# One core: the high part of V's differences moves from ScalarE to GpSimd, and scores are emitted in parts

## Chip, core and metric

The kernel runs on one core of a Trainium2 chip. The time is device microseconds of one execution; the table further down has the median of three runs and the one execution that the profiler recorded. The core's engines work side by side, each through its own queue in order: TensorE (PE in the views; PEld are its weight loads), VectorE (DVE), ScalarE (ACT), GpSimd (POOL) and SyncE (SP), which here issues the DMAs.

## What is computed

A two-layer decoder trunk on 1024 tokens of width 1024: a Mamba-2 layer, then stick-breaking attention with 16 heads of 64, and after each layer a gated per-layer embedding. The change lies in the attention:

```python
z = jnp.einsum('bhtd,bhsd->bhts', q[:, :, q0:kend], k[:, :, :kend])
strict = s_idx < t_idx
log_keep = jnp.where(strict, jax.nn.log_sigmoid(-z), 0.0)
suffix = lax.cumsum(log_keep, axis=3, reverse=True) - log_keep
weights = jnp.where(strict, jnp.exp(jax.nn.log_sigmoid(z) + suffix), 0.0)
outs.append(jnp.einsum('bhts,bhsd->bhtd', weights, v[:, :, :kend]))
```

A weight is the difference of two neighbouring running products of sigmoid(-z). The kernel therefore never forms the weights: it makes the running products (a scan over the keys) and multiplies them with differences of neighbouring rows of V.

## The kernel before

Every matrix product that must be accurate is made of three TensorE products of a high and a low part: a number is rounded to a shorter form (the high part, `...h`), and the rest is the low part (`...l`).

Attention runs over 8 head pairs `hp`, and within a pair over 4 steps p = 3, 2, 1, 0 of 256 tokens each: 32 steps. Tokens are stored in reverse, so the scores of block b run over (8 - b) x 128 keys: 128 and 256 keys at p=3, 384 and 512 at p=2, 640 and 768 at p=1, 896 and 1024 at p=0, for each of the two heads. The steps are pipelined in code order, in `step(i)`:

- *Fill*: for step i, `project` (k, q and v of two token blocks, 24 matmuls each in four groups of six; ScalarE copies k and q out as `kq`, VectorE v as `vr`), and for p=3 and p=2 `gate` (24 matmuls). After these come `values` and `norm`.
- `values` makes V's differences: three DMAs on SP's queue shift `vr` by one row into `vs`, GpSimd subtracts (L853), ScalarE copies the high parts of `V` (L858, two copies of 128x128), GpSimd makes the low parts (L859). `product` reads this V for the first time two steps later.
- `norm` normalizes k and q on VectorE, by a dozen small instructions (`kss`, `krv`, `kry`, `krs`) and a product into `kq` (L870).
- *Pieces*, put between the groups of the fill by their place between 0 and 1: for step i-1 `flip` (four transposes of `kq`, L879, then ScalarE and VectorE write `kst`, `qh`, `ql`) at `FLIP`, and four `scores` spread over `SPREAD[1]`; for step i-2 the turns and products, spread over `SPREAD[0]`. What has a place beyond the last group comes after `values` and `norm`.
- `scores` (L893 to L905): for each half of a wide row, two matmuls into a PSUM tile `z` (two buffers), a sigmoid on ScalarE into `pt` (L903); then one scan over the row on VectorE (L904).
- `turn` (L907): three or four transposes of `pt` on TensorE into a PSUM tile `tr` (L916, L919; two buffers, shared with `flip`), a copy `wh` on ScalarE (L925), a low part `wl` on VectorE (L926). `product` (L936) multiplies both with V; `fold` (L947 to L953) combines the heads into `GT`.

The weights of the next pair are loaded during p=2 and p=1 and split into `g0h` (ScalarE, L104) and `g0l` (VectorE, L108). The order on each engine is the order that a scheduler makes of this code; each engine then runs its own list in order.

Of the kernel before, what the change touches and what calls it, by code (L numbers as in the profile page):

```python
# [8 lines left out]
F32 = mybir.dt.float32  # L9
# [4 lines left out]
ALU = mybir.AluOpType  # L14
# [4 lines left out]
P = 128  # L19
S = 1024  # L20
# [13 lines left out]
NEX = 5  # L34
EARLY = 3
LASTP = ((0, 0, 512), (1, 0, 256), (1, 256, 256))
SPREAD = ((0.05, 0.95), (0.7, 1.0))
FLIP = 0.55
FILL = {32: (7, (4, 5, 6, 7)), 33: (6, ())}
CHUNKS = {30: (0, 1, 2, 3)}  # L40

# [742 lines left out]
def attention(k, A, rawp, hT, oTd, dbg, b2, pairs):  # L784


    tc, nc = k.tc, k.nc
# [3 lines left out]
    with ExitStack() as ctx:  # L791
        pp = ctx.enter_context(tc.tile_pool(name="b_pair", bufs=1, reuse_waits="tile"))
        wk = ctx.enter_context(tc.tile_pool(name="b_work", bufs=2, reuse_waits="tile"))
# [6 lines left out]
        keep = pp.tile([P, S], BF16, name="keep")  # L800
# [7 lines left out]
        def begin_pair(st):  # L808
            st["V"], st["vr"], st["v0"] = {}, {}, {}
            st["GT"] = pairs.gt.tile([P, S], F32, name="GT")  # L810

        def project(st, b):
            W = st["W"]
            ps = mm.tile([P, 512], F32, name="mm")
            prs = []
            sl = slice(b % 4 * P, b % 4 * P + P)
            for kk in range(KT):
                whi, wlo = W[kk]
                prs += terms((hh[b // 4][:, kk, sl], hl[b // 4][:, kk, sl]), (whi[:, :384], wlo[:, :384]))
            yield from split3_some(nc, ps[:, :384], prs, 6)  # L820
            p = b // 2
            if b % 2:
                st["kq"] = wk.tile([P, 2, 2, P], F32, name="kq", bufs=2)
                st["vr"][p] = wk.tile([P, 2, P], F32, name="vr", bufs=3)
            nc.scalar.copy(st["kq"][:, b % 2], ps.rearrange("p (m c) -> p m c", c=256)[:, :, 0:128])
            nc.vector.tensor_copy(st["vr"][p][:, b % 2], ps[:, 128:256])
            yield

        def gate(st, half):
            W = st["W"]  # L830
            gp = mm.tile([P, 512], F32, name="mm")
            sl = slice(half * 512, half * 512 + 512)
            prs = []
            for kk in range(KT):
                whi, wlo = W[kk]
                prs += terms((whi[:, 384:], wlo[:, 384:]), (hh[half][:, kk], hl[half][:, kk]))
            yield from split3_some(nc, gp, prs, 4)
            sg = wk.tile([P, 512], F32, name="sg", bufs=1)
            nc.scalar.activation(sg, gp, AF.Sigmoid)
            nc.vector.tensor_tensor(st["GT"][:, sl], gp, sg, op=ALU.mult)  # L840
            yield

        def values(st, p):

            vr = st["vr"][p]
            vs = wk.tile([P, 2, P], F32, name="vs", bufs=1)
            nc.sync.dma_start(vs[0:P - 1], vr[1:P])
            nc.sync.dma_start(vs[P - 1:P, 0], vr[0:1, 1])
            nc.sync.dma_start(vs[P - 1:P, 1], st["vr"][p + 1][0:1, 0] if p < 3 else zrow)
            st["v0"][p] = sm.tile([P, 2], F32, name="v0", bufs=4)  # L850
            for i in range(2):
                nc.sync.dma_start(st["v0"][p][:, i:i + 1], vr[0:1, i])
            nc.gpsimd.tensor_tensor(vs, vs, vr, op=ALU.subtract)  # L853
            V = st["V"][p] = wk.tile([P, 2, 256], F32R, name="V", bufs=6)
            Vx = V.rearrange("p b (x c) -> p b x c", c=64)
            d = vs.rearrange("p b (h c) -> p b h c", c=64)
            for i in range(2):
                nc.scalar.copy(Vx[:, i, 0::3], d[:, i])  # L858
                nc.gpsimd.tensor_tensor(Vx[:, i, 1:3], d[:, i], Vx[:, i, 0::3].bitcast(F32), op=ALU.subtract)  # L859

        def norm(st, p):
# [11 lines left out]
        def flip(st, p):  # L873
            kn = st.pop(("kn", p))
            tsl = slice(p * 256, (p + 1) * 256)
            tq = trp.tile([P, 512], F32, name="tr")
            for i in range(2):
                for m in range(2):
                    nc.tensor.transpose(tq[:, m * 256 + i * P:m * 256 + (i + 1) * P], kn[:, i, m], ident)  # L879
            kt, qt = tq[:, 0:256], tq[:, 256:512]  # L880
            qh = wk.tile([P, 2, 256], F32R, name="qh", bufs=1)
            for h in range(2):
                o, x = own[h], own[1 - h]
                g = k.gkq[o]
                nc.scalar.activation(kst[o, h, tsl], kt[o], AF.Copy, scale=g)
                nc.vector.scalar_tensor_tensor(
                    kst[x, h, tsl], kt[o], g, kst[o, h, tsl].bitcast(F32), op0=ALU.mult, op1=ALU.subtract)
                nc.scalar.copy(qh[o, h], qt[o])
                nc.scalar.copy(qh[x, h], qt[o])
                nc.vector.tensor_tensor(ql[o, h], qt[o], qh[o, h].bitcast(F32), op=ALU.subtract)  # L890
            st["q", p] = qh

        def scores(st, h, b):  # L893
            qh = st["q", b // 2]
            N = (NT - b) * P
            qs = slice((b % 2) * P, (b % 2) * P + P)
            pt = wk.tile([P, S], F32, name="pt", bufs=5)
            for ko, n in ([(0, N)] if N <= 512 else [(0, N // 2), (N // 2, N // 2)]):
                z = zp.tile([P, 512], F32, name="z")
                rk = kst[:, h, b * P + ko:b * P + ko + n]  # L900
                nc.tensor.matmul(z[:, :n], lhsT=qh[:, h, qs], rhs=rk, start=True, stop=False)
                nc.tensor.matmul(z[:, :n], lhsT=ql[:, h, qs], rhs=rk, start=False, stop=True)
                nc.scalar.activation(pt[:, ko:ko + n], z[:, :n], AF.Sigmoid, scale=-1.0)  # L903
            nc.vector.tensor_tensor_scan(pt[:, :N], pt[:, :N], keep[:, :N], 1.0, op0=ALU.mult, op1=ALU.max)  # L904
            st["a", h, b] = pt  # L905

        def turn(st, p, h, j0):  # L907

# [57 lines left out]
        n = len(steps)  # L966

        def spread(fns, a, z):
            m = len(fns)
            return [(a + (z - a) * (i + 0.5) / m, f) for i, f in enumerate(fns)]  # L970

        def combine_pieces(st, p):

            units = [(h, j) for h in range(2) for j in range(2 * p, NT, 2)]
            def prod(h, j):
                product(st, p, h, j)
                if j == NT - 2:
                    fold(st, p, h)
            fns = []
            for i, (h, j) in enumerate(units):  # L980
                fns.append(lambda h=h, j=j: turn(st, p, h, j))
                if i >= 2:
                    fns.append(lambda u=units[i - 2]: prod(*u))
            return fns + [lambda u=u: prod(*u) for u in units[-2:]]

        def step(i):
            pieces = []
            if i >= 2:
                hp, p = steps[i - 2]
                pieces += spread(combine_pieces(sts[hp], p), *SPREAD[0])  # L990
            if 1 <= i <= n:
                hp, p = steps[i - 1]
                st = sts[hp]
                pieces.append((FLIP, lambda st=st, p=p: flip(st, p)))
                units = [(lambda st=st, h=h, b=b: scores(st, h, b)) for h in range(2) for b in (2 * p + 1, 2 * p)]
                pieces += spread(units, *SPREAD[1])
            pieces.sort(key=lambda x: x[0])
            fill = []
            if i < n:
                hp, p = steps[i]  # L1000
                if p == NT // 2 - 1:
                    pairs.all(hp)
                    begin_pair(sts[hp])
                    if hp + 1 < 8:
                        pairs.start(hp + 1)
                    else:
                        b2.begin(pairs)
                fill = [(project(sts[hp], 2 * p + 1), 5)]
                if p >= 2:
                    fill.append((gate(sts[hp], p - 2), 7))  # L1010
                fill.append((project(sts[hp], 2 * p), 5))
            total = sum(w for _, w in fill)
            done = 0
            for f, w in fill:
                for _ in f:
                    done += 1
                    while pieces and pieces[0][0] <= done / total:
                        pieces.pop(0)[1]()
            if i < n:
                if p in LOADS:  # L1020
                    pairs.step(hp + 1)
                values(sts[hp], p)
                norm(sts[hp], p)
                if i in CHUNKS:
                    b2.weights(CHUNKS[i])
            for _, f in pieces:
                f()
# [226 lines left out]
```

## Time and profile before

| what | value |
|---|---|
| median of 3 runs | 1968.46 us (1967.15 to 1968.69) |
| profiled execution | 1969.7 us |
| its span, first to last instruction | 1968.0 us |
| TensorE busy | 1773.3 us, 90% |
| VectorE busy | 1173.5 us, 60% |
| ScalarE busy | 902.1 us, 46% |
| GpSimd busy | 378.1 us, 19% |
| mean granted TensorE clock | 0.952 |

The span holds the Mamba layer, the embedding, then the attention from some 940 to 1740 us, and the last embedding. Busy shares are means over stages that differ; for the change the attention stage counts alone. A busy TensorE isn't TensorE at its peak: the granted clock says which part of its full speed it had (1.00 is 2.4 GHz, 0.50 is 1.2 GHz). Where a row ends in brackets, the first number in them is the idle time of the engine before that instruction, and behind `<-` stands what ended it.

### The profile page before, as it was taken

To read this page: it belongs to the slowest core of one execution; us is meant where nothing else is said; L and a number is where in the kernel's file an instruction comes from. 1 tells how busy PE (TensorE), PEld (TensorE's weight loads), DVE (VectorE), ACT (ScalarE), POOL (GpSimd) and SP (SyncE) were. 2 spreads that over 40 slices of the span, in tenths; PEclk is the share of its full clock that TensorE was granted. 3 is DMA by queue.
4 is the path that set the end of the run, shared out by engine and by line. 5 is a ranking of instruction groups with operands and counts; after the bars stand their busy time and mean duration, and the time that the engine had idled before them with its cause. 6 is when DMAs were issued, how large, how long until landed. Compare 5 with 4: busy or idle time off the path is not lost.

```text
span 1968.0 us, 25316 instructions
## 1 busy us (share of the span) xinstructions
PE 1773.3 (90%) x9170; PEld 1496.2 (76%) x9170; DVE 1173.5 (60%) x2462; ACT 902.1 (46%) x1974; POOL 378.1 (19%) x384
## 2 busy tenths in 40 slices
PE   7999999999999999999888888888888887679999
PEld 6778878878867778888877777777777776557887
DVE  6685484493596543456476757676767666664332
ACT  5566375375473321244363535353545443542121
POOL 0245445345342222000000000000000001111110
PEclk9999999999999999999989888989898988889999
DMA  4222222232126543222010101010101011223110
GB/s 145 72 84 94 70 86 82 69 93 91 59 92 207 165 144 118 88 86 97 9 57 18 48 17 48 18 47 18 48 18 48 18 37 53 66 86 98 58 49 32
DMA packets 96396, 139.41 MB, mean 71 GB/s; under 512 B 18160, under 2 KB 66640, under 8 KB 96272
## 3 DMA queue, kind: packets, MB, share of 16 engines
q1 hardware_dynamic: 96272, 137.80, 21.8%
q8 instruction: 72, 1.18, 0.2%
q14 instruction: 52, 0.43, 0.1%
HBM read 108.77 MB, written 24.77 MB: 68 GB/s over the span
## 4 chain that ended last, share of the span: by engine, by line
PE 61%; DMA 15%; DVE 13%; ACT 7%; issue 2%; POOL 2%; POOLq 0%; SPq 0%; DVEq 0%; ACTq 0%
PE mm L46 38%; DMA vs<-vr 13%; PE mm L53 9%; DVE pt L904 3%; PE pq L46 2%; PE oq L936 2%; DVE v L234 2%; PE intra L409 2%; PE tr L916 1%; DVE wl L926 1%; POOL vs L853 1%; PE inter L404 1%; PE tr L664 1%; ACT pt L903 1%; PE tr L919 1%
## 5 line engine op out<-in xcount | busy, mean ns | idle before, releaser
L46 PE MATMUL mm<-ul,wh 128*128 128x512 f32 (+1 forms) x648 | 254.0, 392 | 0.0
L46 PE MATMUL mm<-uh,wl 128*128 128x512 f32 (+1 forms) x648 | 252.5, 390 | 0.0
L46 PE MATMUL mm<-uh,wh 128*128 128x512 f32 (+1 forms) x648 | 252.4, 389 | 0.1
L904 DVE TENSOR_TENSOR_SCAN pt<-pt,keep 128x128 f32<-128x128 f32 (+7 forms) x128 | 175.4, 1374 | 55.3 <-ACT pt L903 54.9
L53 PE MATMUL mm<-g0h,hh 128*128 128x384 f32 x512 | 191.4, 374 | 3.6 <-ACT g0h L104 2.9
L53 PE MATMUL mm<-g0l,hh 128*128 128x384 f32 x512 | 179.4, 350 | 1.9 <-DVE g0l L108 1.9
L53 PE MATMUL mm<-g0h,hl 128*128 128x384 f32 x512 | 179.0, 350 | 0.0
L916 PE MATMUL tr<-ident,pt 128*128 128x128 f32 x320 | 82.6, 306 | 104.7 <-DVE wl L926 102.2
L926 DVE TENSOR_TENSOR wl<-tr,wh 128x512 fp32r<-128x512 f32 (+1 forms) x160 | 101.3, 634 | 121.5 <-ACT wh L925 119.1
L234 DVE SCALAR_TENSOR_TENSOR v<-u,convh,v 128x512 f32<-128x512 f32 x144 | 130.1, 909 | 55.1 <-ACT v L232 52.6
L853 POOL TENSOR_TENSOR vs<-vs,vr 128x256 f32<-128x256 f32 x32 | 23.3, 728 | 682.7 <-DMA vs<-vr 654.8
L925 ACT CAST wh<-tr 128x512 fp32r<-128x512 f32 (+1 forms) x160 | 85.0, 543 | 126.2 <-PE tr L919 124.6
L46 PEld LDWEIGHTS mm<-ul,wh 128*128 128x128 f32 x648 | 121.7, 188 | 26.4 <-issue 2.3
L46 PEld LDWEIGHTS mm<-uh,wl 128*128 128x128 f32 x648 | 121.8, 188 | 25.7 <-issue 1.9
L46 PEld LDWEIGHTS mm<-uh,wh 128*128 128x128 f32 x648 | 121.7, 188 | 25.4 <-issue 1.1
L916 PEld LDWEIGHTS tr<-ident,pt 128*128 128x128 f32 x320 | 48.1, 154 | 118.9 <-DVE wl L926 110.4
L106 POOL TENSOR_TENSOR wl<-raw,wh 128x1024 fp32r<-128x1024 f32 x39 | 95.3, 2443 | 155.6 <-ACT wh L104 148.9
L53 PEld LDWEIGHTS mm<-g0h,hh 128*128 128x128 f32 x512 | 101.3, 198 | 4.5 <-ACT g0h L104 3.2
L53 PEld LDWEIGHTS mm<-g0l,hh 128*128 128x128 f32 x512 | 101.9, 199 | 2.8 <-DVE g0l L108 2.1
L858 ACT CAST V<-vs 128x128 fp32r<-128x128 f32 x64 | 15.9, 295 | 191.7 <-POOL vs L853 191.7
L53 PEld LDWEIGHTS mm<-g0h,hl 128*128 128x128 f32 x512 | 101.6, 198 | 0.6
L574 DVE SCALAR_TENSOR_TENSOR acc<-mm,rg,acc 128x512 f32<-128x512 f32 x64 | 47.7, 748 | 84.1 <-PE mm L46 83.3
(350 smaller groups left out, 4427.6 us busy)
## 6 DMA issues: line engine op xcount, KB each, us to landing
raw<-in_w_in SPq DMA_DIRECT2D x40, 512.0 KB
ex<-acd SPq DMA_DIRECT2D x64, 256.0 KB
raw<-in_w_b SPq DMA_DIRECT2D x32, 512.0 KB
raw<-in_m_out SPq DMA_DIRECT2D x16, 512.0 KB
raw<-in_gate SPq DMA_DIRECT2D x16, 512.0 KB
graw<-gT SPq DMA_DIRECT2D x30, 256.0 KB
gT<-zs SPq DMA_DIRECT2D x28, 256.0 KB
acc<-in_x SPq DMA_DIRECT2D x8, 512.0 KB
```

The source lines that it names most:

```text
L46: nc.tensor.matmul(out, lhsT=a, rhs=b, start=(i == 0), stop=(i == n - 1))
L53: nc.tensor.matmul(out, lhsT=a, rhs=b, start=(i == 0), stop=(i == n - 1))
L106: (eng or nc.gpsimd).tensor_tensor(lo, raw, hi.bitcast(F32), op=ALU.subtract)
L234: nc.vector.scalar_tensor_tensor(vv, u[:, 3 - j:3 - j + 512], w(j), vv, op0=ALU.mult, op1=ALU.add)
L409: nc.tensor.matmul(aq[hp * 64:hp * 64 + 64, jp * 256 + i * P:jp * 256 + (i + 1) * P], lhsT=xdts[2 * qt + i][:, (2 * j + hp) * 64:(2 * j + ...
L574: nc.vector.scalar_tensor_tensor(acc[:, sl], ps, k.rg[:, g, t:t + 1], acc[:, sl], op0=ALU.mult, op1=ALU.add)
L853: nc.gpsimd.tensor_tensor(vs, vs, vr, op=ALU.subtract)
L904: nc.vector.tensor_tensor_scan(pt[:, :N], pt[:, :N], keep[:, :N], 1.0, op0=ALU.mult, op1=ALU.max)
L916: nc.tensor.transpose(tq[:, c:c + P], al[:, i0:i0 + P], ident)
L925: nc.scalar.copy(wh[:, :c], tq[:, :c])
L926: nc.vector.tensor_tensor(wl[:, :c], tq[:, :c], wh[:, :c].bitcast(F32), op=ALU.subtract)
L936: nc.tensor.matmul(out[:, :w], lhsT=st["V"][j // 2][:, j % 2, h * P:(h + 1) * P], rhs=rhs, start=(j0 == 2 * p and i == 0), stop=(j0 == NT ...
```

## The change

Three things are edited, all in `attention` and its constants. ScalarE's copy of V's high parts becomes a GpSimd copy. `scores` no longer emits a whole row at once but returns its parts (up to 512 keys each), so that a wide row's halves get places of their own; the row's scan is emitted with its last part. `FLIP` goes from 0.55 to 0.5, and the scores' spread begins at 0.62 in place of 0.7.

```diff
-SPREAD = ((0.05, 0.95), (0.7, 1.0))
-FLIP = 0.55
+SPREAD = ((0.05, 0.95), (0.62, 1.0))
+FLIP = 0.5
...
             for i in range(2):
-                nc.scalar.copy(Vx[:, i, 0::3], d[:, i])
+                nc.gpsimd.tensor_copy(Vx[:, i, 0::3], d[:, i])
                 nc.gpsimd.tensor_tensor(Vx[:, i, 1:3], d[:, i], Vx[:, i, 0::3].bitcast(F32), op=ALU.subtract)
...
         def scores(st, h, b):
-            qh = st["q", b // 2]
+
             N = (NT - b) * P
             qs = slice((b % 2) * P, (b % 2) * P + P)
-            pt = wk.tile([P, S], F32, name="pt", bufs=5)
-            for ko, n in ([(0, N)] if N <= 512 else [(0, N // 2), (N // 2, N // 2)]):
+            parts = [(0, N)] if N <= 512 else [(0, N // 2), (N // 2, N // 2)]
+            def part(i):
+                qh = st["q", b // 2]
+                if i == 0:
+                    st["a", h, b] = wk.tile([P, S], F32, name="pt", bufs=5)
+                pt = st["a", h, b]
+                ko, n = parts[i]
                 z = zp.tile([P, 512], F32, name="z")
...
-            nc.vector.tensor_tensor_scan(pt[:, :N], pt[:, :N], keep[:, :N], 1.0, op0=ALU.mult, op1=ALU.max)
-            st["a", h, b] = pt
+                if i == len(parts) - 1:
+                    nc.vector.tensor_tensor_scan(pt[:, :N], pt[:, :N], keep[:, :N], 1.0, op0=ALU.mult, op1=ALU.max)
+            return [lambda i=i: part(i) for i in range(len(parts))]
...
-                units = [(lambda st=st, h=h, b=b: scores(st, h, b)) for h in range(2) for b in (2 * p + 1, 2 * p)]
+                units = [f for h in range(2) for b in (2 * p + 1, 2 * p) for f in scores(st, h, b)]
```

How this moves instructions shows at three places. Lines from 893 on stand up to six further down in the changed kernel.

ScalarE, where the scores of a pair's step p=0 end and the turns of p=1 begin, before:

```order
L903 ACTIVATE pt<-z 128x512 x2
L903 ACTIVATE pt<-z 128x448 x2
L947 COPY of<-oq 64x256
L903 ACTIVATE pt<-z 128x512
L858 CAST V<-vs 128x2x64 x2
L903 ACTIVATE pt<-z 128x512
L925 CAST wh<-tr 128x384
L925 CAST wh<-tr 128x512
```

ScalarE at the same place of the changed kernel:

```order
L908 ACTIVATE pt<-z 128x512
L908 ACTIVATE pt<-z 128x448 x2
L953 COPY of<-oq 64x256
L908 ACTIVATE pt<-z 128x512 x2
L931 CAST wh<-tr 128x384
L931 CAST wh<-tr 128x512
```

The V copy stood ahead of the row's last sigmoid and of the `wh` copies, and is gone from this queue; on GpSimd's queue it now stands between L853 and L859.

VectorE at the same step, from the second scan to the `wl` of the first turn, before:

```order
L904 SCALAR_TENSOR_TENSOR pt<-pt,keep 128x1024
L75 TENSOR_SCALAR kry<-kry 128x8
L904 SCALAR_TENSOR_TENSOR pt<-pt,keep 128x896
L77 TENSOR_TENSOR krs<-kry,krv 128x8
L948 TENSOR_TENSOR of<-oq,of 64x256
L78 SCALAR_TENSOR_TENSOR krs<-krs,kry 128x8
L904 SCALAR_TENSOR_TENSOR pt<-pt,keep 128x1024
L79 SCALAR_TENSOR_TENSOR kry<-krs,kry 128x8
L953 SCALAR_TENSOR_TENSOR GT<-of,v_10603,GT 128x128
L77 TENSOR_TENSOR krs<-kry,krv 128x8
```

VectorE there in the changed kernel:

```order
L910 SCALAR_TENSOR_TENSOR pt<-pt,keep 128x1024
L85 TENSOR_SCALAR krv<-kss 128x8
L910 SCALAR_TENSOR_TENSOR pt<-pt,keep 128x896
L74 TENSOR_SCALAR kry<-krv 128x8
L954 TENSOR_TENSOR of<-oq,of 64x256
L75 TENSOR_SCALAR kry<-kry 128x8
L910 SCALAR_TENSOR_TENSOR pt<-pt,keep 128x1024
L77 TENSOR_TENSOR krs<-kry,krv 128x8
L959 SCALAR_TENSOR_TENSOR GT<-of,v_10609,GT 128x128
```

The scans keep their order, the norm's small steps fall two places behind them; in both kernels the second GT product, small steps and `wl` follow.

VectorE at the step p=1, from the last scan on, before:

```order
L904 SCALAR_TENSOR_TENSOR pt<-pt,keep 128x768
L77 TENSOR_TENSOR krs<-kry,krv 128x8
L926 TENSOR_TENSOR wl<-tr,wh 128x384
L78 SCALAR_TENSOR_TENSOR krs<-krs,kry 128x8
L108 SCALAR_TENSOR_TENSOR g0l<-raw,kvn,g0h 128x256
```

VectorE there in the changed kernel:

```order
L910 SCALAR_TENSOR_TENSOR pt<-pt,keep 128x768
L77 TENSOR_TENSOR krs<-kry,krv 128x8
L959 SCALAR_TENSOR_TENSOR GT<-of,v_10429,GT 128x128
L78 SCALAR_TENSOR_TENSOR krs<-krs,kry 128x8
L959 SCALAR_TENSOR_TENSOR GT<-of,v_10429,GT 128x128
L79 SCALAR_TENSOR_TENSOR kry<-krs,kry 128x8
L108 SCALAR_TENSOR_TENSOR g0l<-raw,kvn,g0h 128x256
L77 TENSOR_TENSOR krs<-kry,krv 128x8
L932 TENSOR_TENSOR wl<-tr,wh 128x384
```

Two GT products (before: ahead of the scan) and a weight's low part now stand between the last scan and `wl`.

## Rows read from the trace of the kernel before

**Rows 1.** The page's part 4, the chain that ended last, by line.

```profile
PE mm L46 38%; DMA vs<-vr 13%; PE mm L53 9%; DVE pt L904 3%; PE pq L46 2%; PE oq L936 2%; DVE v L234 2%; PE intra L409 2%; PE tr L916 1%; DVE wl L926 1%; POOL vs L853 1%; PE inter L404 1%; PE tr L664 1%; ACT pt L903 1%; PE tr L919 1%
```

**Rows 2.** Waits, 950 to 1800: who waited for whom, us, times, longest.

```profile
ACT V L858 <- POOL vs L853: 191.7, 32, 8.7
...
PE tr L916 <- DVE wl L926: 102.2, 24, 6.3
...
PE tr L879 <- DVE kq L870: 9.9, 2, 5.8
PE z L901 <- ACT pt L903: 9.8, 19, 1.0
```

**Rows 3.** The chain in order of time, 1126 to 1146: start, us, what.

```profile
1127.90 7.91 DMA vs<-vr
...
1137.75 2.37 DVE pt L904
...
1140.89 0.57 DVE wl L926
```

**Rows 4.** Timeline of ScalarE, 1126 to 1146.

```profile
1136.73 0.50 ACT L858 CAST V<-vs 128x128 fp32r<-128x128 f32 x2 [6.12 <-POOL vs L853]
```

**Rows 5.** Stretches by head pair: length, busy (PE, PEld, DVE, ACT, POOL), PEclk, DMA.

```profile
944.50:1030.30 85.80, 71.64 (x379) 64.99 (x377) 54.65 (x137) 41.31 (x103) 6.38 (x12) 0.90 0.13 37
1030.30:1127.80 97.50, 80.44 (x456) 73.36 (x456) 65.74 (x152) 47.58 (x115) 6.38 (x12) 0.91 0.11 33
...
1325.80:1424.70 98.90, 82.07 (x457) 74.86 (x456) 65.87 (x151) 47.73 (x115) 6.38 (x12) 0.90 0.11 33
...
1523.70:1622.60 98.90, 82.18 (x457) 74.95 (x456) 63.23 (x143) 44.50 (x107) 6.39 (x12) 0.90 0.09 27
```

**Rows 6.** Stretches around the pause of rows 3, the same columns.

```profile
1126.00:1135.20 9.20, 9.20 (x53) 8.01 (x51) 7.62 (x11) 4.01 (x8) 0.00 (x0) 1.00 0.05 14
1139.40:1146.20 6.80, 4.70 (x15) 4.08 (x16) 4.67 (x15) 0.59 (x1) 0.00 (x0) 0.50 0.02 3
```

**Rows 7.** Timelines, VectorE and TensorE, before two pauses: start, us, engine, line.

```profile
1104.02 0.34 DVE L953 SCALAR_TENSOR_TENSOR GT<-of,v,GT 128x128 f32<-128x128 f32 x1
...
1105.87 0.39 PE L53 MATMUL mm<-hh,g0h 128*128 128x512 f32 x1
...
1133.61 0.17 DVE L78 SCALAR_TENSOR_TENSOR krs<-krs,kry 128x8 f32<-128x8 f32 x1
...
1134.92 0.34 PE L53 MATMUL mm<-g0h,hl 128*128 128x384 f32 x1
```

**Rows 8.** VectorE by form, 1226.8 to 1325.8: busy us, mean ns, idle before.

```profile
L904 DVE TENSOR_TENSOR_SCAN pt<-pt,keep 128x1024 f32<-128x1024 f32 x2 | 4.6, 2324 | 4.0 <-ACT pt L903 4.0
...
L108 DVE SCALAR_TENSOR_TENSOR g0l<-raw,sn,g0h 128x256 fp32r<-128x256 f32 x8 | 3.8, 478 | 0.0
L904 DVE TENSOR_TENSOR_SCAN pt<-pt,keep 128x768 f32<-128x768 f32 x2 | 3.5, 1752 | 2.8 <-ACT pt L903 2.8
...
L904 DVE TENSOR_TENSOR_SCAN pt<-pt,keep 128x256 f32<-128x256 f32 x2 | 1.4, 682 | 0.0
```

**Rows 9.** GpSimd by line, the whole span: busy us, mean ns, idle before.

```profile
L859 POOL TENSOR_TENSOR V<-vs,V 128x128 fp32r<-128x128 f32 x64 | 27.8, 456 | 12.6 <-ACT V L858 12.6
...
L802 POOL CAST keep<-tri 128x128 bf16<-128x128 f32 x1 | 0.3, 291 | 0.0
```

**Rows 10.** Timelines of GpSimd and VectorE, 1653 to 1662.

```profile
1655.05 2.41 POOL L106 TENSOR_TENSOR hl<-raw,hh 128x1024 fp32r<-128x1024 f32 x1 [22.18 <-ACT hh L104]
...
1655.55 2.45 DVE L904 TENSOR_TENSOR_SCAN pt<-pt,keep 128x256 f32<-128x256 f32 x1
```

**Rows 11.** Stretches between two of the norm's reductions, columns as rows 5.

```profile
1127.80:1160.20 32.40, 26.16 (x150) 23.65 (x150) 19.13 (x38) 12.56 (x29) 1.59 (x3) 0.89 0.02 5
...
1177.40:1197.70 20.30, 16.33 (x95) 15.49 (x94) 16.73 (x41) 13.30 (x32) 1.59 (x3) 0.92 0.19 59
1197.70:1226.80 29.10, 25.41 (x135) 22.40 (x133) 19.80 (x43) 14.70 (x37) 1.61 (x3) 0.88 0.13 41
```

## Prediction

> **What bounds the kernel now.** I read the page first. In its chain that ended last, the line that is not TensorE work and yet stands second is the DMA `vs<-vr`, 13% of the span [rows 1]. The waits between 950 and 1800 us then say who sits behind it [rows 2]: ScalarE waits 191.7 us, 32 times, at L858 for GpSimd's subtraction L853, which waits for that DMA; and TensorE waits 102.2 us, 24 times, at the transposes of L916 for VectorE's L926. The chain in order of time ties the two together at one of the 32 places [rows 3]: DMA 7.91 us, L853, L858, a sigmoid, then VectorE's scan 2.37 us, `wl` 0.57 us, and the transpose on TensorE. In ScalarE's own row the V copy ends 6.12 us of idling [rows 4]. So the copy itself (0.5 us for two) is cheap; it is dear because ScalarE's queue runs in order and the sigmoids and `wh` copies that TensorE needs stand behind a copy whose input is still on its way. V itself is wanted only a step later.
>
> The stretches by head pair give the size [rows 5]. Six pairs run from 1030.3 to 1622.6, 592.3 us, 98.7 each; in one TensorE is busy 82.0 to 82.2 of 98.9, idle 17, and its mean granted clock is 0.90. The clock goes with the idling [rows 6]: 1.00 (2.4 GHz) over 1126 to 1135.2, where TensorE had no pause, and 0.50 (1.2 GHz) over 1139.4 to 1146.2, which begins in the pause that the chain of [rows 3] ends; there it was busy 4.70 of 6.80 us. A mean of 0.90 over 98.9 us is 9.9 us of full clock not granted; a third of such a stretch is idle, so about 8 of them cost work. At full clock and without pauses a pair has 82 - 8 = 74 us of TensorE work. That is the floor under this change: 24.7 us less per pair.
>
> **The change, part by part.** *ScalarE loses L858*: 64 copies, and with them every wait behind the DMA. Nothing else on ScalarE reads `vs` or V in this stage, and the new order of its queue holds no instruction on V. What is next late at each place is the rest of VectorE's queue, from its rows.
>
> Everywhere the transposes that wait are those of the third turn of a step: a turn's PSUM tile has two buffers, and the third turn needs the one that the first turn's `wl` reads last. Step p=0 of a pair (the scans of 1024 keys): VectorE is free at 1133.61 + 0.17 = 1133.78 [rows 7], the last scan takes 2.32 on the mean [rows 8], from its end to the start of `wl` the chain shows 1140.89 - (1137.75 + 2.37) = 0.77, then `wl` 0.57 [rows 3]. That puts the transpose at 1137.4. TensorE runs dry at 1134.92 + 0.34 = 1135.26 [rows 7]. A pause of 2.2 us stays of the 6.3 that is the longest today [rows 2]. The new order keeps the scan, GT, `wl` sequence, so the earlier and finer score parts give nothing at this place.
>
> Step p=1 (768 keys): VectorE is free at 1104.02 + 0.34 = 1104.36 [rows 7], the scan 1.75 [rows 8] and `wl` 0.57 end at 1106.7; TensorE runs dry at 1105.87 + 0.39 = 1106.26. Some 0.4 stays, and the new order sets a weight's low part, 0.48 [rows 8], ahead of `wl`: 1.0 in all. Step p=2 has shorter scans: I take 0.8, between 0 and the 2.2 of the longest.
>
> *GpSimd gains the copies*, two per step. No GpSimd row has this very form; its subtraction of 128x128 takes 456 ns and its one cast of 128x128 (to another type) 291 [rows 9]: two cost 0.58 to 0.91. Beside 6.4 us of GpSimd work in 99 us [rows 5] that is nothing for GpSimd itself, and V has a full step to come before it is read. It may cost VectorE: a scan of 256 keys took 2.45 us while GpSimd ran a subtraction of 2.41 [rows 10], against 682 ns alone [rows 8]; so GpSimd can hold VectorE up for its whole instruction. Today its work begins when VectorE, too, waits for ScalarE. Afterwards the DMA lands while VectorE is in its scans. A step's GpSimd work is 6.4 / 4 = 1.6, with the copies 2.2 to 2.5 us; at p=0 it starts some 9 us after `vr`, today at 1136, which is where the scan would now end. I charge 0.8 there (0 to 2.5), for about a third of it can meet the operations that stand between the scan and `wl`.
>
> The Trainium skill, "SBUF — State Buffer", section "Who interferes with whom", speaks against this placing: GpSimd and VectorE share one pair of ports, and a VectorE instruction with two SBUF inputs and a GpSimd instruction that reads SBUF exclude each other for a whole instruction. The 2.45 us scan agrees. By the page's rule the copies, read as GpSimd instructions, would cost VectorE their full length wherever it is at a scan; the second rival is that case.
>
> *Flip earlier (0.55 to 0.5), scores from 0.62 and in parts.* TensorE gets the same matmuls; halves of a wide score now stand apart with projections between them. The waits of z for a sigmoid are small today (9.8 us in all [rows 2]), so this gains under 0.3 a pair. The flips come one group of six projection matmuls earlier, and ahead of a flip the norm chain must have ended on VectorE. I take 0.8 a pair: 0 if it has, and at the dear end 5.8 a flip, the longest such wait in the trace [rows 2]. On SP's queue only the order of a few weight loads and one-row copies changes by a place or two; they are ahead of need by a step, so I take nothing.
>
> **The sum for a pair.** Work 74; pauses 2.2 + 0.8 + 1.0 + 0.8 + 0.8 and 1.4 for the remaining small waits (17.0 idle today less the large gaps), 7.0; clock 3 instead of 8, since pauses of 2 to 3 us remain once or twice a pair. 84.0, so 14.7 saved, six times: 88. The first pair (944.5 to 1030.3) has 85.8 - 71.6 = 14.2 idle at clock 0.90 [rows 5]: with 6 idle and 2.5 for the clock it saves 12. The last pair has the same four ScalarE waits but ends in a stretch whose other waits stay; 14. Together 114, from the profiled execution's 1969.7 (its span 1968.0): 1855.7. The median of the runs is 1968.46, 1.2 lower: 1854.
>
> **The rivals.** *Nearly all comes back.* VectorE's 66 us a pair fit under 74, GpSimd's work falls beside operations that read PSUM, and the clock stays at 1.00. A pair then takes 74 + 3 = 77; 6 x 21.7 + 15 + 20 = 165 less: 1803. For it: VectorE has 33 of 99 us free. Against: the 2.2 at p=0 follows from durations alone.
>
> *VectorE becomes the bound, held up by GpSimd.* By step [rows 11]: in the stretch 1177.4 to 1197.7 VectorE has 16.73 of work and TensorE 16.33 at clock 0.92, some 14.7 at full clock. With 2.3 of GpSimd's time on top VectorE needs 19.0, 4.3 more than TensorE; in the next stretch 19.8 + 2.3 = 22.1 against 25.41 less 3.5, 21.9: level; in the longest TensorE leads, 26.16 less 3.6 against 19.13 + 2.3. So 74 + 4.3 + 7 + 3 = 88.3 a pair, 10.4 saved, 62, and 18 for the ends: 80 less, 1888.
>
> *Slower: flips wait for the norm.* The flip stands ahead of projections and scores in TensorE's queue, in order, and VectorE now does scans before the norm's small steps. Were each of the four flips a pair 5.8 us late, as the one in the trace, with today's clock: 74 + 7 + 23 + 8 = 112, 13 more per pair, about 80 in all, 2048. It decides from (24.7 - 7 - 8) / 4 = 2.4 us a flip. Against it: one such wait in 32 flips is of this size now, and the flips move by no more than one group of six matmuls.
>
> That the change does not do what it says is excluded: the copies are on GpSimd's queue in the new order.
>
> **How the numbers follow.** Forecast 0.60, all back 0.15, VectorE bound 0.21, slower 0.04. What this kernel's measurement can tell from no change is about 0.2%, 4 us; none of the cases lands there except in passing: 0.01. The forecast's own bounds, from the ends of the unknown costs, are 1825 to 1880. The range takes in both neighbours, 1803 to 1893, and leaves out the slower case and the tails. Faster 0.95, same 0.01, slower 0.04.
>
> **What would show it.** Right: no ScalarE wait on L853; ScalarE's idling ends at TensorE; a pair of 80 to 88 us; granted clock 0.95 or more over pairs; the longest pause left at the transposes of p=0's step, 2 to 4 us, ended by `wl`. The GpSimd term: scans of 1024 keys well over 2.32 us. The flip term: waits at L879 for `kq`. Wrong: pairs still above 92 us, or pauses that end on GpSimd's V.

## The result, and the profile after

The changed kernel takes 1832.84 us (median of four runs, 1831.58 to 1836.15), the kernel before 1968.58 in the runs beside it (1967.15 to 1968.91). The ratio is 0.9314 with a 95% interval of 0.9298 to 0.9331: 135.7 us less, where the prediction said 1854 and thus 114. The profiled execution has a span of 1831.1 us at a mean granted clock of 0.985; before it was 1968.0 at 0.952.

Part 4 of the profile page, the chain that ended last by line, is the first thing to hold against [rows 1]:

```profile
PE mm L46 41%; PE mm L53 11%; DVE pt L910 7%; PE pq L46 2%; PE oq L942 2%; DVE v L234 2%; PE intra L409 2%; PE tr L922 1%; DVE g0l L108 1%; DVE wl L932 1%; PE inter L404 1%; PE tr L664 1%; ACT pt L908 1%; PE tr L925 1%; PE tr L388 1%
```

The DMA `vs<-vr`, 13% before, is in the list no more. In its place VectorE's scan (`pt`, L910) has grown from 3% to 7%. The waits between 940 and 1650 us (who waited for whom: us, times, longest) answer to [rows 2]:

```profile
POOL vs L853 <- DMA vs<-vr: 324.9, 17, 26.2
...
ACT wh L931 <- PE tr L925: 143.9, 91, 3.7
...
PE tr L922 <- DVE wl L932: 26.6, 21, 4.4
...
PE z L906 <- ACT pt L908: 11.0, 18, 1.1
PE z L906 <- ACT qh L889: 9.3, 8, 3.5
```

ScalarE's 191.7 us behind GpSimd are gone. GpSimd still waits for the DMA, for 324.9 us, but nothing that anybody needs soon stands behind it. ScalarE now waits for TensorE (`wh` for the transposes), as it should. TensorE's wait for `wl` fell from 102.2 us to 26.6; its waits for scores (`z`) are 11.0 and 9.3.

The stretches by head pair answer to [rows 5], with its columns (length, busy PE, PEld, DVE, ACT, POOL, PEclk, DMA):

```profile
944.50:1014.30 69.80, 64.62 (x378) 58.74 (x377) 55.70 (x137) 40.04 (x95) 9.90 (x20) 1.00 0.15 46
1014.30:1095.00 80.70, 75.05 (x458) 68.43 (x458) 67.83 (x151) 46.66 (x107) 9.54 (x20) 1.00 0.13 40
...
1177.20:1259.50 82.30, 76.71 (x459) 69.89 (x458) 67.77 (x151) 46.65 (x107) 9.29 (x20) 0.98 0.12 39
...
1423.60:1503.90 80.30, 75.13 (x458) 68.28 (x457) 64.82 (x142) 43.72 (x99) 9.63 (x20) 1.00 0.10 34
...
1503.90:1831.10 327.20, 294.69 (x1417) 243.73 (x1415) 165.44 (x359) 108.75 (x220) 41.83 (x40) 0.94 0.20 66
```

The six steady pairs run from 1014.3 to 1503.9, 489.6 us or 81.6 each, where they took 592.3 or 98.7. That is 102.7 us of the 136.9 by which the span fell. The first pair gave 16.0 (85.8 to 69.8), what follows the six pairs 18.2 (345.4 to 327.2). TensorE now idles 5.5 us a pair on the mean instead of 17, at a clock of 1.00 or 0.98 instead of 0.90. VectorE's work rose from 66 to 67.8 us, GpSimd's from 6.4 to 9.3.

One pause is left in each pair that is longer than 2 us, at step p=0, where the prediction put it. The timeline of TensorE, VectorE and GpSimd there (start, us, engine, line):

```profile
1182.74 2.28 DVE L910 TENSOR_TENSOR_SCAN pt<-pt,keep 128x1024 f32<-128x1024 f32 x1
...
1184.21 0.34 PE L53 MATMUL mm<-g0h,hl 128*128 128x384 f32 x1
...
1184.95 0.73 POOL L853 TENSOR_TENSOR vs<-vs,vr 128x256 f32<-128x256 f32 x1 [20.88 <-DMA vs<-vr]
1184.99 0.83 DVE L959 SCALAR_TENSOR_TENSOR GT<-of,v,GT 128x128 f32<-128x128 f32 x1
1185.74 0.61 POOL L858 CAST V<-vs 128x128 fp32r<-128x128 f32 x2
...
1185.82 0.38 DVE L959 SCALAR_TENSOR_TENSOR GT<-of,v,GT 128x128 f32<-128x128 f32 x1
...
1186.40 0.56 DVE L932 TENSOR_TENSOR wl<-tr,wh 128x384 fp32r<-128x384 f32 x1
...
1187.01 0.45 PE L922 MATMUL tr<-ident,pt 128*128 128x128 f32 x1 [2.47 <-DVE wl L932]
```

VectorE goes from scan to scan without idling; nothing in its queue waits for a sigmoid. It has more to do there than TensorE has cover for, and one of its instructions is drawn out beside GpSimd's subtraction (L853): here a GT product, 0.83 us, and so in four of the seven pauses at this place. In the other three, as in the first pair, the GT products keep their 0.34 and a small step of the norm (`krs`) takes 0.68:

```profile
1022.13 0.85 POOL L853 TENSOR_TENSOR vs<-vs,vr 128x256 f32<-128x256 f32 x1 [23.13 <-DVE krs L77]
1022.32 0.68 DVE L78 SCALAR_TENSOR_TENSOR krs<-krs,kry 128x8 f32<-128x8 f32 x1
```

### The profile page after: what moved, and what is told of

Same layout as the page of the kernel before. It is cut to its first block, busy times and chain, and to the rows that moved or that the text cites. A ratio compares the mean times of both kernels' runs of the same rounds, so it can differ in the third digit from the quotient of the medians.

```text
span 1831.1 us, 25275 instructions
## 1 busy us (share of the span) xinstructions
PE 1730.8 (95%) x9170; PEld 1455.5 (79%) x9170; DVE 1190.6 (65%) x2462; ACT 893.8 (49%) x1910; POOL 402.2 (22%) x448
## 4 chain that ended last, share of the span: by engine, by line
PE 68%; DVE 20%; ACT 7%; DMA 2%; issue 2%; POOL 0%; SPq 0%; DVEq 0%; ACTq 0%
PE mm L46 41%; PE mm L53 11%; DVE pt L910 7%; PE pq L46 2%; PE oq L942 2%; DVE v L234 2%; PE intra L409 2%; PE tr L922 1%; DVE g0l L108 1%; DVE wl L932 1%; PE inter L404 1%; PE tr L664 1%; ACT pt L908 1%; PE tr L925 1%; PE tr L388 1%
## 5 line engine op out<-in xcount | busy, mean ns | idle before, releaser
L53 PE MATMUL mm<-g0h,hh 128*128 128x384 f32 x512 | 182.5, 357 | 0.0
L910 DVE TENSOR_TENSOR_SCAN pt<-pt,keep 128x128 f32<-128x128 f32 (+7 forms) x128 | 175.8, 1377 | 0.8 <-ACT pt L908 0.3
L53 PE MATMUL mm<-g0l,hh 128*128 128x384 f32 x512 | 172.7, 337 | 2.5 <-DVE g0l L108 2.5
L53 PE MATMUL mm<-g0h,hl 128*128 128x384 f32 x512 | 172.9, 338 | 0.0
L853 POOL TENSOR_TENSOR vs<-vs,vr 128x256 f32<-128x256 f32 x32 | 24.3, 760 | 546.0 <-DMA vs<-vr 324.9
L922 PE MATMUL tr<-ident,pt 128*128 128x128 f32 x320 | 75.2, 283 | 29.3 <-DVE wl L932 26.6
L53 PEld LDWEIGHTS mm<-g0l,hh 128*128 128x128 f32 x512 | 96.8, 189 | 4.1 <-DVE g0l L108 3.1
L53 PEld LDWEIGHTS mm<-g0h,hh 128*128 128x128 f32 x512 | 96.5, 189 | 0.7
L53 PEld LDWEIGHTS mm<-g0h,hl 128*128 128x128 f32 x512 | 96.4, 188 | 0.6
L647 DVE SCALAR_TENSOR_TENSOR pth<-pth,pq 128x512 f32<-128x512 f32 (+1 forms) x33 | 22.2, 672 | 111.9 <-PE pq L46 107.2
L908 ACT ACTIVATE pt<-z 128x320 f32<-128x320 f32 (+3 forms) x192 | 89.8, 490 | 10.0 <-PE z L907 8.1
```

Of the source, the lines that this page charges most:

```text
L53: nc.tensor.matmul(out, lhsT=a, rhs=b, start=(i == 0), stop=(i == n - 1))
L922: nc.tensor.transpose(tq[:, c:c + P], al[:, i0:i0 + P], ident)
```

## The experiments

Twelve kernels were run. They ask three things: which of the edits counts, whether it was ScalarE's work or its waiting, and what holds the time that is left. Each ratio is to the kernel before, run beside it, with a 95% interval.

### Which edit counts

**The copy alone** (the kernel before with one line changed):

```diff
-                nc.scalar.copy(Vx[:, i, 0::3], d[:, i])
+                nc.gpsimd.tensor_copy(Vx[:, i, 0::3], d[:, i])
```

> The kernel before with one line changed: the high part of V is copied on GpSimd; the places and the wholeness of the scores stay. Theory (ScalarE's wait behind the shifted copy of v is the cost, the new places are worth little): 1825 to 1860 us, ScalarE waits on GpSimd gone, pairs of 81 to 85 us, a pause of 2 to 3 us left at the step with 1024 keys. Rival (the finer scores and the earlier flip carry a good part of the 136 us): 1880 us or more.

Measured: 1845.46 us (1840.13 to 1851.84), ratio 0.9377 (0.9351 to 0.9402), span 1838.4. That lies in the range of the theory. The copy alone brings 123 of the 136 us.

**The order alone** (the changed kernel with the copy back on ScalarE):

```diff
-                nc.gpsimd.tensor_copy(Vx[:, i, 0::3], d[:, i])
+                nc.scalar.copy(Vx[:, i, 0::3], d[:, i])
```

> The changed kernel with the copy of V's high part back on ScalarE: parts, earlier flip and earlier scores alone. Theory: within 10 us of 1968, ScalarE still waits some 190 us on GpSimd and TensorE's four pauses a pair stay. Rival (the order carries part of the gain): below 1940.

Measured: 1979.44 us, ratio 1.0057 (1.0039 to 1.0075), 11 us slower than the kernel before, just outside the 10 us of the theory. Its waits between 940 and 1750 us:

```profile
ACT V L858 <- POOL vs L853: 207.9, 32, 8.7
...
PE tr L922 <- DVE wl L932: 106.0, 23, 6.0
...
PE tr L879 <- DVE wl L932: 21.5, 6, 3.8
```

The new places don't shorten the wait behind the DMA (207.9 against 191.7). One flip a pair (L879) waits behind `wl`, and this pause grew: in the kernel before it was

```profile
PE tr L879 <- DVE wl L926: 12.6, 6, 2.2
```

The likely reading is that a flip that stands earlier meets the held-up queue sooner. At 1.5 us, six times, that is 9 of the 11. So the 13 us that the order gives in the changed kernel are to be had only once the copy is gone from ScalarE.

**The new places, with a wide row's two halves again emitted together**:

```diff
-                units = [f for h in range(2) for b in (2 * p + 1, 2 * p) for f in scores(st, h, b)]
+                units = [(lambda st=st, h=h, b=b: [f() for f in scores(st, h, b)]) for h in range(2) for b in (2 * p + 1, 2 * p)]
```

> The changed kernel with each row of scores emitted whole again, at the new places (flip 0.5, scores from 0.62). With the first run (copy alone: 1845) and the changed kernel (1833) it parts the 13 us of the new order in two. Theory (the halves set apart do it, since two z tiles take turns with the sigmoids): 1838 to 1850 us, more waits of z for the sigmoid. Rival (the earlier places do it): within 5 us of 1833.

Measured: 1830.98 us (1828.55 to 1834.36), ratio 0.9307 (0.9291 to 0.9322). That is the time of the whole change, against the theory: the 13 us come from `FLIP` and `SPREAD`, and the splitting of the rows gives nothing. Where the 13 us lie, the profiles show in part. The profiled execution with the copy alone is the fastest of its four, so the two spans (1838.4 and 1831.1) differ by 7.3 only. Cut at the same instruction as [rows 5] (the norm's reduction that opens a pair), the six steady pairs with the copy alone are

```profile
1014.40:1506.40 492.00, 455.27 (x2737) 416.81 (x2736) 402.40 (x893) 276.50 (x629) 59.22 (x120) 0.99 0.12 38
```

or 82.0 us each against 81.6: 2.4 us in all. The first pair takes 71.0 against 69.8, and what follows the six pairs 332.0 against 327.2; the stage starts 1.1 earlier there. Around the last pair, 1500 to 1640 us, the kernel with the copy alone has these waits on TensorE,

```profile
PE tr L916 <- DVE wl L926: 15.1, 6, 5.6
PE tr L879 <- DVE kq L870: 6.0, 1, 6.0
```

where the changed kernel has

```profile
PE tr L922 <- DVE wl L932: 7.1, 3, 4.4
...
PE tr L879 <- DVE kq L870: 2.6, 2, 1.4
```

The wait for `kq` is that of 5.8 us of [rows 2]; little is gained by its fall, since the scores behind this flip now wait 3.5 us for `qh`, which the flip writes. The larger part is the turns' wait for `wl`. The other 5 us between the medians are not placed.

This kernel also tells what GpSimd's subtraction costs at p=0, for there it falls elsewhere, and no VectorE instruction is drawn out:

```profile
1186.85 0.34 DVE L959 SCALAR_TENSOR_TENSOR GT<-of,v,GT 128x128 f32<-128x128 f32 x1
1187.12 0.16 DVE L78 SCALAR_TENSOR_TENSOR krs<-krs,kry 128x8 f32<-128x8 f32 x1
...
1188.66 0.33 PE L922 MATMUL tr<-ident,pt 128*128 128x128 f32 x1 [1.96 <-DVE wl L932]
```

The pause is 1.96 to 2.01 us in all seven places, where the changed kernel has 2.47 to 2.54. VectorE's small steps lie a little differently too, so the half microsecond goes to GpSimd by the nearest comparison, not by a clean one.

### Work or wait

**The copy on VectorE** instead of GpSimd:

```diff
-                nc.gpsimd.tensor_copy(Vx[:, i, 0::3], d[:, i])
+                nc.vector.tensor_copy(Vx[:, i, 0::3], d[:, i])
```

> The changed kernel with the copy of V's high part on VectorE. Theory (the copy's place in an in-order queue that TensorE depends on is the cost): VectorE takes over the wait on GpSimd, 100 us or more in all, and the time goes back to 1920 to 2010 us. Rival (what counts is that ScalarE has less to do): 1835 to 1865.

Measured: 2033.31 us, ratio 1.0329 (1.0314 to 1.0345). The direction was expected, the size was not (1920 to 2010 was the range): 65 us slower than before and 200 slower than the change. The waits between 940 and 1750 us:

```profile
DVE V L858 <- POOL vs L853: 150.5, 31, 6.0
...
PE tr L922 <- DVE wl L932: 118.9, 20, 6.2
...
PE tr L879 <- DVE wl L932: 33.9, 6, 5.8
```

The same small copy now blocks VectorE's queue, with the scans, `wl` and the norm behind it. TensorE waits longer for `wl` than before the change, at the turns (118.9 us against 102.2) and at the flips (33.9 against 12.6), and its mean granted clock is 0.940 against 0.952.

**The copy on ScalarE, emitted a step later.** V's differences and their parts are set apart from `values` and emitted after the next step's work, when the DMA should long have landed:

```diff
+            st["vs"] = vs, vr
+
+        def values2(st, p):
+            vs, vr = st.pop("vs")
...
-                nc.gpsimd.tensor_copy(Vx[:, i, 0::3], d[:, i])
+                nc.scalar.copy(Vx[:, i, 0::3], d[:, i])
...
+                if i:
+                    values2(sts[steps[i - 1][0]], steps[i - 1][1])
```

> The changed kernel, but V's differences, high part (on ScalarE again) and low part are emitted one step later, when the shifted copy has long landed; V is still ready ahead of its first product. ScalarE has all its old work, without the wait. Theory (the wait and not the work was the cost): 1822 to 1850 us. Rival (ScalarE is short of time, or the move to GpSimd is needed): over 1865. GpSimd's subtraction then meets other VectorE work.

Measured: 1978.76 us, ratio 1.0048 (1.0032 to 1.0064), a miss. The trace shows why: the program's scheduler put the copy back to the place that it had in ScalarE's queue. The waits between 940 and 1750 us are those of the order alone:

```profile
ACT V L862 <- POOL vs L857: 206.8, 32, 8.8
```

So this kernel did not try what it was made for, and it tells nothing about work or wait.

**The copy on ScalarE, with nothing to wait for.** The parts are made of `vr`, which is there without the DMA. This leaves the difference of rows out of V, so the kernel tells of the time alone:

```diff
-            d = vs.rearrange("p b (h c) -> p b h c", c=64)
+            d = vr.rearrange("p b (h c) -> p b h c", c=64)
...
-                nc.gpsimd.tensor_copy(Vx[:, i, 0::3], d[:, i])
+                nc.scalar.copy(Vx[:, i, 0::3], d[:, i])
```

> The changed kernel with the high part's copy back on ScalarE, but V's parts are made of v itself (vr), which is on the core already, and not of the shifted difference: the DMAs and the subtraction still run, but nothing on ScalarE waits for them. So V is not the difference of rows here. ScalarE has its 64 copies as before, without the wait. Theory (the wait was the cost, not the copies and not the engine): 1822 to 1848 us and no ScalarE wait on GpSimd. Rival (ScalarE is short of time): over 1865.

Measured: 1833.98 us (1831.88 to 1836.01), ratio 0.9321 (0.9304 to 0.9338), the time of the changed kernel. ScalarE's waits from 937 to 1575 us:

```profile
ACT wh L931 <- PE tr L925: 118.2, 80, 3.3
ACT V L858 <- DVE vr L826: 37.3, 24, 3.6
```

ScalarE makes all 64 copies, at about 0.3 us each, and still waits 37.3 us for VectorE's `vr`; yet the time is that of the kernel in which it makes none. With the same order and the late input ScalarE's copies took 1979.44 us (the order alone). So what cost the time was not ScalarE's work but the place of a late input in its queue.

**More work on GpSimd.** Each copy is made four times there, 192 copies more:

```diff
-                nc.gpsimd.tensor_copy(Vx[:, i, 0::3], d[:, i])
+                for _ in range(4):
+                    nc.gpsimd.tensor_copy(Vx[:, i, 0::3], d[:, i])
```

> The changed kernel with every copy of V's high part made four times on GpSimd: 192 copies more, some 60 us of GpSimd time, all between the subtraction and the low parts. Theory (GpSimd holds VectorE up where it meets instructions with both inputs in SBUF, and that matters only at the step with 1024 keys): scans and small VectorE steps beside it get longer, the pause there grows from 2.5 to 3 to 4.5 us, 1838 to 1862 us. Rival (GpSimd's place is free of cost): within 5 us of the changed kernel. Rival (VectorE as the bound, each GpSimd microsecond paid in full): 1875 or more.

Measured: 1832.91 us (1831.2 to 1835.49), ratio 0.9321 (0.9306 to 0.9335): no cost, as one rival had it. The theory, 1838 to 1862 us with a longer pause, falls. The timeline at p=0's pause:

```profile
1184.83 0.72 POOL L853 TENSOR_TENSOR vs<-vs,vr 128x256 f32<-128x256 f32 x1 [18.27 <-DMA vs<-vr]
1184.87 0.83 DVE L960 SCALAR_TENSOR_TENSOR GT<-of,v,GT 128x128 f32<-128x128 f32 x1
1185.62 2.04 POOL L859 CAST V<-vs 128x128 fp32r<-128x128 f32 x8
...
1185.70 0.38 DVE L960 SCALAR_TENSOR_TENSOR GT<-of,v,GT 128x128 f32<-128x128 f32 x1
...
1186.28 0.56 DVE L933 TENSOR_TENSOR wl<-tr,wh 128x384 fp32r<-128x384 f32 x1
1186.75 0.21 DVE L77 TENSOR_TENSOR krs<-kry,krv 128x8 f32<-128x8 f32 x1
...
1186.89 0.33 PE L923 MATMUL tr<-ident,pt 128*128 128x128 f32 x1 [2.47 <-DVE wl L933]
```

A GT product beside the subtraction takes 0.83 us, the next one, beside the casts, 0.38 (0.34 with GpSimd idle), and `wl` its 0.56 as in the changed kernel. The casts are eight instructions of some 0.3 us each, with VectorE's instructions coming in between; the norm's small steps beside them take 0.20 or 0.21 where the rows of the new places alone have 0.16. So a cast draws VectorE out by a few hundredths of a microsecond, and the pause is 2.47 as in the changed kernel.

### What is left

**Half the scan.** Each scan goes over the first half of its row, so the running products of the other half are left out:

```diff
-                    nc.vector.tensor_tensor_scan(pt[:, :N], pt[:, :N], keep[:, :N], 1.0, op0=ALU.mult, op1=ALU.max)
+                    nc.vector.tensor_tensor_scan(pt[:, :N // 2], pt[:, :N // 2], keep[:, :N // 2], 1.0, op0=ALU.mult, op1=ALU.max)
```

> The changed kernel with each scan cut to the first half of its row, so the running products of the other half are left out: VectorE has some 88 us less. Theory (the pause that is left at the step with 1024 keys is VectorE's backlog of scans): that pause goes, pairs fall from 82 to 77 to 79 us, 1790 to 1815 us. Rival (the pauses left come from GpSimd's holding VectorE up, or from the score buffers): over 1822.

Measured: 1783.92 us (1782.3 to 1784.57), ratio 0.9069 (0.9056 to 0.9083), 6 us below the range that was expected. The pair that answers to 1177.2 of the changed kernel, in the columns of [rows 5]:

```profile
1160.30:1236.20 75.90, 74.02 (x458) 68.55 (x457) 57.77 (x151) 46.43 (x107) 9.57 (x20) 1.00 0.14 42
```

With 10 us less on VectorE the pause at p=0 is gone, the clock is 1.00, and the pair takes 75.9 us with 74.0 of TensorE work in it. So the rest of the pair, 82.3 less 75.9, goes when VectorE has less to do.

**Three buffers for the turns' transposes**, paid for with one of the two for their products:

```diff
-        trp = ctx.enter_context(tc.tile_pool(name="b_tr", bufs=2, space=PSUM, reuse_waits="tile"))
-        op = ctx.enter_context(tc.tile_pool(name="b_o", bufs=2, space=PSUM, reuse_waits="tile"))
+        trp = ctx.enter_context(tc.tile_pool(name="b_tr", bufs=3, space=PSUM, reuse_waits="tile"))
+        op = ctx.enter_context(tc.tile_pool(name="b_o", bufs=1, space=PSUM, reuse_waits="tile"))
```

> The changed kernel with three PSUM buffers for the turns in place of two, and one for the products in place of two. Theory (VectorE's backlog is what is late, the buffer only says at which turn TensorE meets it): within 12 us of the changed kernel, the pause moves to a later turn or to the products that wait for the fold. Rival (the buffers are the limit): under 1815.

Measured: 1815.9 us (1813.98 to 1816.36), ratio 0.9231 (0.9217 to 0.9245), 17 us below the changed kernel. The theory had it within 12, the rival under 1815, so neither hit. The pair, and the pause at p=0, in this kernel:

```profile
1171.80:1250.50 78.70, 74.85 (x459) 68.79 (x458) 67.83 (x151) 46.75 (x108) 9.31 (x20) 1.00 0.13 41
```

```profile
1181.64 0.44 PE L942 MATMUL oq<-wl,V 128*128 128x256 f32 x2 [0.95 <-DVE wl L932]
```

The third turn no longer waits for the first one's buffer; what waits now is the product that reads `wl` itself, 0.95 us instead of 2.47, and the clock stays at 1.00. VectorE's work is unchanged (67.83 us), yet the pair is 3.6 us shorter: two buffers are a limit here too, beside VectorE's backlog. Among the kernels that leave nothing out it is the fastest, with the next but one, which cannot be told from it.

**The same, with the flip still earlier** (0.4):

```diff
-FLIP = 0.5
+FLIP = 0.4
```

> Three PSUM buffers for the turns, one for the products (1816 us) and the flip at 0.4 in place of 0.5: at the step with 640 and 768 keys one more group of projections and a product stand between flip and scores. Theory (the 1.4 us wait of z for the flip's copies there is a latency that work in between can cover): that wait goes, 1800 to 1813 us. Rival (the norm chain is then late and the flip waits): 1816 or more, with waits of the flip for the normalized kq.

Measured: 1822.77 us, ratio 0.927 (0.9256 to 0.9283), 7 us slower than with 0.5: the rival's case. The flip of a step now comes before its norm is done, as here:

```profile
1219.83 0.63 PE L879 MATMUL tr<-ident,kq 128*128 128x128 f32 x4 [1.53 <-DVE kq L870]
```

**The same, with the scores earlier too** (`FLIP` 0.4 and the spread from 0.55):

```diff
-SPREAD = ((0.05, 0.95), (0.62, 1.0))
-FLIP = 0.5
+SPREAD = ((0.05, 0.95), (0.55, 1.0))
+FLIP = 0.4
```

> As the run before it, and scores from 0.55 in place of 0.62, so that the first scan of each step starts earlier. Theory (VectorE's scan backlog is what the turns wait for, and it starts earlier): the waits at the 1024-key step vanish, 1795 to 1812 us. Rival (VectorE's queue is full anyway, and the flip's copies come too late for the earlier scores): no faster than that run, with z waiting for qh.

Measured: 1815.26 us (1810.5 to 1816.98), ratio 0.9227 (0.9213 to 0.9242), as with three buffers alone, and neither in the range of the theory (up to 1812) nor without gain on the kernel just above, as the rival had it. In the steady pairs the wait at the step of 1024 keys vanishes, and the flips wait for the norm instead, 3.2 us in one pair.

**Three buffers in the kernel before.**

> The kernel before, with three PSUM buffers for the turns and one for the products: ScalarE still copies V's high part. Theory (ScalarE's queue stands still for some 6 us a step, and one more turn under way covers little of it): 1940 to 1966 us, the ScalarE wait on GpSimd still over 150 us. Rival (the buffers alone would have done it): below 1900.

Measured: 1920.12 us (1919.61 to 1921.71), ratio 0.9766 (0.9751 to 0.978). Both sides missed: one had 1940 to 1966, the other under 1900. The wait itself is untouched,

```profile
ACT V L858 <- POOL vs L853: 190.8, 32, 8.8
```

but one more turn under way covers part of it for TensorE, 47 us in all. The whole change, which removes the wait, was worth 136.

## Why the prediction was right, point by point

**The cause** was read rightly, and is now shown from three sides: without the copy in that queue the 191.7 us and the DMA in the chain are gone; with the copy back they return (207.9 us, 1979 us); with the copy there but its input early (1834 us), the time is as good as without it. The step that the argument hung on, that V itself is wanted a step later and GpSimd's queue has nothing urgent, holds as well: no pause in the pairs ends on GpSimd's V.

**The pair.** Forecast 74 of work, 7.0 of pauses and 3 for the clock, 84.0. Over the six pairs TensorE is busy 76.1 of 81.6 us. In the two pairs at a clock of 1.00 it is busy 75.1, so work is 75 (1 over the forecast), pauses are 5.5 (1.5 under) and the clock costs 1.0 on the mean (2 under): 2.4 us a pair less than forecast, 14 of the 23 us by which the span came out below the forecast. The terms missed both ways, work and small waits too low by 1.1 and 0.8, the others too high by some 4.3 together, so part of the closeness is luck.

- *Work*: of the 9.9 us of clock not granted, a third idle leaves 6.6, not the 8 that was taken off; by the rows themselves (4.70 busy of 6.80) it is 6.8, and 82 less 6.8 is 75.2, which is what was measured. The 74.0 of the kernel with half the scans is near the forecast's 74, but comes from other work on VectorE and does not bear the sum out.
- *p=0's pause*: forecast 2.2 and 0.8 for GpSimd, 3.0; measured 2.47. GpSimd's share is about 0.5: one VectorE instruction drawn out by the subtraction, by 0.5 in either form, with little from the copies that the change added. That leaves 2.0 for the base, and 2.0 is the pause where the subtraction falls elsewhere (the new places alone).
- *p=1's and p=2's pauses*: forecast 1.0 and 0.8; measured 0.45 and 0.36 in the pair from 1177.2. Both sizes were too large by half. The weight's low part that now stands ahead of `wl` costs its place, but VectorE probably comes there earlier than the timeline of before showed, since it no longer waits for sigmoids; no run takes this apart.
- *Flips*: charged at 0.8; no flip waits in the steady pairs, and the earlier places of flips and scores together gained 13 us over the whole stage. The term had the wrong sign.
- *Small waits for scores*: forecast 1.4 in all for the rest; the waits of `z` alone are 0.81, 1.09 and 0.25, 2.2 in the pair. The 0.81 is for `qh`, which the flip writes. Here the sum was too low.
- *Clock*: forecast 3, because pauses of 2 to 3 us remain. The row shows less: one stretch of 3.4 us at half clock in four of the six pairs, 1.7 us each, and none in the other two.

**The ends.** The first pair gave 16.0 where 12 was forecast, what follows the six pairs 18.2 where 14 was. The first pair idles 5.2 us, nearly as was said (6), but its clock costs nothing, where 2.5 stood in the sum. The 14 had no sum of its own behind it.

**The rivals.** *Nearly all comes back* (1803) lay 30 us below, the forecast 21 above: VectorE's rest at p=0 stands nearly as computed, and the pair reaches 76 only with shorter scans, 78.7 with three buffers. *VectorE held up by GpSimd* (1888) is refuted by size: the pair takes 81.6 and not 88.3, and 192 more copies on GpSimd change nothing. The sign that was named for it, scans of 1024 keys well over 2.32 us, is absent; they take 2.28. But GpSimd's work overlaps these scans by at most 0.07 us, since it starts as the scan ends, where the prediction had placed it. That GpSimd can hold up a scan shows near the end of the stage, where one of 768 keys, 1.75 us elsewhere, takes 3.17 beside a subtraction:

```profile
1567.22 2.55 POOL L106 TENSOR_TENSOR hl<-raw,hh 128x1024 fp32r<-128x1024 f32 x1 [5.29 <-ACT hh L104]
...
1568.21 3.17 DVE L910 TENSOR_TENSOR_SCAN pt<-pt,keep 128x768 f32<-128x768 f32 x1 [0.30 <-ACT pt L908]
```

The Trainium skill, "SBUF — State Buffer", section "Who interferes with whom", was cited for a GpSimd instruction that reads SBUF excluding a two-input VectorE instruction for its whole length. The trace agrees for GpSimd's subtraction (GT 0.83 us beside it, 0.34 without), and the run with four-fold copies does not speak against it: there each cast is an instruction of some 0.3 us of its own, so that by this rule VectorE waits for one cast at most, and the GT product in their midst took 0.38. What failed of that rival is the place, for the copies meet small steps and not scans, and so the size.

*Flips wait for the norm* (2048) did not happen with the flip at 0.5, but is a real mechanism: at 0.4, with three buffers, the flips wait for `kq`, the time is 7 us longer, and earlier scores give these back.

## What to carry to other kernels

When a cheap instruction has a late input, look at what stands behind it in its engine's queue, not at its duration: in the new order the 64 small copies cost 147 us on ScalarE and 200 on VectorE against GpSimd (1979, 2033 and 1833 us), because only on GpSimd nothing behind them was urgent. Before such a move, work out what comes second at each place that waited, from the next engine's durations; here this gave the pause that stayed to within half a microsecond. And once the large wait is gone, try the small edits again: the new places lost 11 us with the wait in place and gave 13 without it.

## What the runs showed of the hardware that was not expected

The same pause did not have the same effect on the clock. In the pair from 1014.3 the transpose waits 2.48 us and the clock stays at 1.00; in the pair from 1177.2 it waits 2.47, and what follows runs at half clock (1.2 GHz) for some 3.4 us:

```profile
1024.08 0.33 PE L922 MATMUL tr<-ident,pt 128*128 128x128 f32 x1 [2.48 <-DVE wl L932]
```

```profile
1184.60:1187.00 2.40, 0.00 (x0) 0.00 (x0) 2.37 (x8) 0.35 (x1) 1.99 (x5) 1.00 0.00 0
1187.00:1188.10 1.10, 1.09 (x5) 1.09 (x6) 0.93 (x6) 0.00 (x0) 0.19 (x1) 0.53 0.00 0
1188.10:1190.00 1.90, 1.90 (x8) 1.51 (x6) 1.90 (x5) 0.59 (x1) 0.00 (x0) 0.50 0.01 0
```

The clock is still 1.00 through the pause itself, 1184.6 to 1187.0, and falls with the first transposes after it. With the copy alone, a pause of 2.68 us at this place, which ends at 1106.57, is followed by full clock, and the 3.4 us at half clock come at 1153.2, after three short waits of 0.94, 0.26 and 0.79 us. Why it falls after the one pause and not after the other stays open.

A VectorE instruction that meets GpSimd's subtraction can come out several times as long: a step of the norm on 128x8 numbers went from 0.16 to 0.68 us, a GT product from 0.34 to 0.83, and both ended within 0.15 us after the subtraction.
